# Attention scores as full-height products of stacked q and k, the mask within the row maximum, scores negated

## The chip, the cores and the metric

The kernel runs on one core of a Trainium2 chip. The metric is the device time of one execution in microseconds (us); for the kernel before, three timed executions gave a median of 1242.78 us (1242.35 to 1244.48). One further execution was taken with the hardware profiler; its own time was 1240.29 us. All rows below come from it. Engines are called TensorE (PE in the rows, PEld for its weight loads), VectorE (DVE), ScalarE (ACT), GpSimd (POOL) and SyncE (SP, which issues the transfers).

## The reference

The input is x, 512 positions by 1024 features, float32. Two layers follow, each an attention and a feed-forward network (SwiGLU, 2816 hidden features), each of these closed by `x <- LayerNorm(alpha * x + sublayer(x))`.

Layer A is differential attention with rotary positions: 8 heads, and in each head two maps of 64 features that share one value of 128 features.

```python
q = apply_rope(q, cos, sin) * (A_HEAD_DIM ** -0.5)
k = apply_rope(k, cos, sin)
sc = einsum('bqhmd,bkhmd->bhmqk', q[:, q0:kend], k[:, :kend])
allowed = chunk_id[None, :kend] <= chunk_id[q0:kend, None]      # chunks of 64
p = softmax(where(allowed, sc, neg), axis=-1)
a = p[:, :, 0] - lam * p[:, :, 1]
```

`a` is multiplied by the values, normalised (RMS) and projected. Layer B is chunked attention of 16 heads with 64 features; with 512 positions its band of nine chunks holds every key up to the end of the query's own chunk. A learned bias by relative distance is added to its scores before the softmax.

## The kernel before, in words

All float32 operands of the matrix products are split into a high part that TensorE takes (`F32R`) and a low part, what is left; a product is then high x high + high x low + low x high, three matmuls that add into one PSUM bank. The features lie on the partitions for q and k (128 of them: the two maps of a head of A, or two heads, a pair, of B), the positions along the free dimension.

The kernel has six stages one after the other: values and q, k of the first head; attention A; feed-forward 0; first projections of B; attention B; feed-forward 1. In either attention stage there are 32 units: 8 heads (or pairs, in B), each with 4 query tiles of 128 positions. A unit (`unit_a`, L978, and `unit_b`, L1218) makes the scores of both maps into a pair of PSUM banks (`scores`, L817), the row maximum (`top`), the exponential with its sum (`ex`), in A the combination of both maps (`mix`) and in B the division (`norm`), transposes the result on TensorE (banks of the tag `sm`) and multiplies it with the values.

Scores: a map has 64 features, so its q and k take half the partitions. `scores` runs over the three products and in each over the two maps, so that a matmul on partitions 0 to 63 and one on 64 to 127 follow one another, into two banks. A query tile reads keys up to its own end, but at least 256 columns: 256, 256, 384 and 512 for the four tiles. In A two more matmuls with one partition (`ind`, `negrow`) add a large negative number to the last 64 keys for the first 64 queries. In B the bias tile holds it already, and a fused VectorE instruction adds the bias, writes the sum to `e` and takes the maximum; a multiplication by -1 follows.

q and k of a head come from a projection (`qk_a`, L868: 24 matmuls of 512 columns each; `qk_b`, L1126). In A, `rope` copies the projection to `r`, swaps the halves with four transfers to `sw`, multiplies with cosine and sine, adds, and then `high` (ScalarE) and `low` (VectorE) write `qh`, `ql` or `kh`, `kl`; this last part begins when the units of the head before have begun. In B, `split_` does the two steps directly from PSUM; the bank (tag `pj`, two of them) is free when `low` has read it, and the output projection `o_proj` takes the same two banks when the projections are done.

Order of the work. Each engine executes its instructions in the order in which this program issues them, and a planner decides that order: `Modelled` and `Model` (L58, L97) keep an estimated clock for each engine and the estimated time at which each block of a tile is ready. `chain` issues a step on another engine when its inputs are estimated to be ready. `weave` (L243) interleaves the attention's steps with fill work, that is projections of later heads, values and the output projection: at each `fill` step a set time's worth of it (`FA`, `FB`), and, where a step waits for `there(...)`, as much as is estimated to pass until the tiles are there. In A the fill rates of the last three units are nearly zero. Weights come in chunks of 512 KB by SP (`fetch`, five raw buffers) and are split by ScalarE and VectorE (some by GpSimd) two chunks ahead of use.

Of the kernel before, what the change touches and what calls it, by code (L numbers as in the profile page):

```python
# [19 lines left out]
P = 128  # L20
S = 512
# [111 lines left out]
def trunk(ctx, tc, x, a_w_qkv, a_lambda, a_subln_g, a_w_o, kv_w, b_w_q, b_rel_bias, b_w_o,  # L133
# [212 lines left out]
    def fetch():  # L346

        i = state["raw"]
        if i < len(order):
            src, shape, _ = plan[order[i]]  # L350
            raws[i] = new(wraw, NRAW, [P] + shape, F32, "raw", f"raw_{order[i]}")
            load_e.dma_start(raws[i], src)
            state["raw"] += 1
# [463 lines left out]
    def scores(sc, q, k, qt, mask=True):  # L817
        kend = (qt + 1) * P
        N = max(kend, 256)
        qs = slice(qt * P, (qt + 1) * P)  # L820
        for i, (a, b) in enumerate(((0, 0), (0, 1), (1, 0))):
            for m in range(2):
                ms = slice(m * 64, (m + 1) * 64)
                mm(sc[m][:, :N], q[a][ms, qs], k[b][ms, :N], start=(i == 0), stop=(i == 2 and not mask))
        for m in range(2 if mask else 0):
            mm(sc[m][:, kend - 64:kend], ind, negrow, start=False, stop=True)
# [23 lines left out]
    ind = ap1.tile([1, P], BF16, name="ind")  # L850
    vec_e.memset(ind[:, 0:64], 1.0)
    vec_e.memset(ind[:, 64:P], 0.0)
    negrow = ap1.tile([1, 64], BF16, name="negrow")
    vec_e.memset(negrow, NEG)
# [13 lines left out]
    def qk_a(h):  # L868
# [4 lines left out]
        def rope(nm, scale, ps):  # L873
# [7 lines left out]
            out = {}  # L881

            def add():
                vec_e.tensor_add(rc, rc, sw)

            def high():
                out["h"] = new(ap2, 2, [P, S], F32R, nm + "h", f"{nm}h_{h}")
                act_e.activation(out["h"], rc, AF.Copy, scale=scale)

            def low():  # L890
                out["l"] = new(ap2, 2, [P, S], F32R, nm + "l", f"{nm}l_{h}")
                vec_e.scalar_tensor_tensor(out["l"], rc, scale, out["h"].bitcast(F32), op0=ALU.mult,
                                           op1=ALU.subtract)
# [13 lines left out]
        for nm, scale in (("q", SCALE), ("k", 1.0)):  # L907
# [4 lines left out]
            rope(nm, scale, ps)  # L912
# [65 lines left out]
    def unit_a(h, qt):  # L978
# [3 lines left out]
        q, k = qk[h]  # L982
        sc = pair(f"sc_{n_}")
        scores(sc, q, k, qt)
# [54 lines left out]
    def attention_a():  # L1039
# [3 lines left out]
        for i in range(nu + max(step[1] for step in STEPS if step[0] != "fill")):  # L1043
            rates = FA[0] if i < FA[2] else FA[1] if i < nu else FA[3]
            for kind, n in STEPS:
# [6 lines left out]
                if kind == "s":  # L1052
                    yield lambda: h in qk
                    yield lambda: there(*qk[h][0], *qk[h][1])
# [69 lines left out]
    oTl = oTp.tile([P, KT, S], F32R, name="oTl1")  # L1124

    def qk_b(p):  # L1126

        parts = [("bq", SCALE), ("bk", 1.0)]
        res = []

        def split_(nm, scale, ps):
            hi = new(bp2, 2, [P, S], F32R, nm + "h", f"{nm}h_{p}")
            lo = new(bp2, 2, [P, S], F32R, nm + "l", f"{nm}l_{p}")
            chain([hi, lo, ps], (lambda: [ps], lambda: act_e.activation(hi, ps, AF.Copy, scale=scale)), (
                lambda: [hi], lambda: vec_e.scalar_tensor_tensor(
                    lo, ps, scale, hi.bitcast(F32), op0=ALU.mult, op1=ALU.subtract)))
            res.append((hi, lo))

        if p == 0:
            ws = [take(f"{nm}{p}") for nm, _ in parts]  # L1140
            pss = [bank("pj", f"{nm}_ps_{p}") for nm, _ in parts]
# [234 lines left out]
```

## Time and profile before

| what | us |
|---|---|
| median of three runs (lowest to highest) | 1242.78 (1242.35 to 1244.48) |
| the profiled execution, its own time | 1240.29 |
| its span, first to last instruction | 1238.5 |
| TensorE busy | 1204.0 |
| VectorE busy | 888.7 |
| ScalarE busy | 526.3 |
| GpSimd busy | 454.6 |

The span lies inside the execution's time. A matmul's shown duration includes its way through the array, and matmuls overlap, so what a matmul costs is read from the distance between its start and the next start, not from its duration. A row of the timeline merges like instructions that follow one another without a gap; "x2" is their number, the second column the time from the first one's start to the last one's end.

### The profile page before, as it was taken

Reading aid. Unit: us, or ns where it says so; the run is one execution under the profiler, and the core shown is the slowest. Engines: PE = TensorE matmul, PEld = TensorE weight load, DVE = VectorE, ACT = ScalarE, POOL = GpSimd, SP = SyncE. Lnnn points to the kernel's source line nnn. Section 1 sums busy time; section 2 is a strip of 40 time slices with the busy share of each in tenths; the row PEclk is TensorE's granted clock in tenths of the full one; section 3 lists DMA queues with packets and bytes.
Section 4 is the critical chain, followed back from the end, with each engine's and each line's share of the span. In section 5 each row is a group of like instructions: output and inputs, shape, how many; then the busy total and the mean of one; then the engine's idle time right before and its main releaser. Section 6 shows DMA issues by size and latency. Waiting matters only on the chain.

```text
span 1238.5 us, 20141 instructions
## 1 busy us (share of the span) xinstructions
PE 1204.0 (97%) x7832; PEld 1070.5 (86%) x7832; DVE 888.7 (72%) x1386; ACT 526.3 (42%) x1009; POOL 454.6 (37%) x408
## 2 busy tenths in 40 slices
PE   8999999999999999999999999999999999999997
PEld 7878887788999999888897888878889999998886
DVE  4587576489999999432655677776899999983327
ACT  4356555333444444322235565563344444443220
POOL 0135333417666663001213232313186666620022
PEclk9999999899999999999999999999999999999999
DMA  8433222443554444523243222225423443353321
GB/s 263 112 87 108 65 75 85 150 128 94 151 143 136 134 125 136 171 88 133 85 137 115 73 86 86 69 86 187 120 68 107 118 117 103 103 174 116 102 68 68
DMA packets 161631, 141.56 MB, mean 114 GB/s; under 512 B 5584, under 2 KB 136944, under 8 KB 161536
## 3 DMA queue, kind: packets, MB, share of 16 engines
q1 hardware_dynamic: 161536, 140.28, 37.3%
q8 instruction: 61, 1.00, 0.3%
q14 instruction: 34, 0.28, 0.1%
HBM read 127.63 MB, written 13.67 MB: 114 GB/s over the span
## 4 chain that ended last, share of the span: by engine, by line
PE 81%; DVE 8%; POOL 4%; issue 3%; ACT 2%; DMA 1%; SPq 0%; DVEq 0%; POOLq 0%; ACTq 0%
PE m L194 29%; PE a L194 5%; PE b L194 5%; PE c L194 5%; PE d L194 4%; PE va_ps L194 4%; PE k_ps L194 3%; PE q_ps L194 3%; PE bq_ps L194 3%; PE vb_ps L194 2%; PE bk_ps L194 2%; PE sc L194 2%; POOL ha L75 2%; PE ob L194 2%; POOL sums L75 2%
## 5 line engine op out<-in xcount | busy, mean ns | idle before, releaser
L75 POOL TENSOR_TENSOR lo_fo<-raw_fo,hi_fo 128x1024 fp32r<-128x1024 f32 x8 | 19.1, 2392 | 215.4 <-ACT hi_fo L75 215.4
L75 POOL TENSOR_TENSOR sums<-raw_u 128x512 f32<-128x512 f32 x38 | 50.9, 1340 | 119.9 <-DVE s3lo L75 119.9
L75 DVE TENSOR_TENSOR lo_fk<-raw_fk,hi_fk 128x1024 fp32r<-128x1024 f32 x28 | 33.9, 1224 | 66.4 <-ACT hi_fk L75 66.4
L75 POOL TENSOR_TENSOR sums<-raw_g,raw_u 128x512 f32<-128x512 f32 x38 | 77.7, 2044 | 0.0
L75 ACT ACTIVATE sg<-sg 128x512 f32<-128x512 f32 x38 | 24.0, 633 | 125.9 <-DVE sg L75 125.9
L75 ACT CAST s3hi<-sums 128x1024 fp32r<-128x1024 f32 x38 | 40.0, 1052 | 77.2 <-POOL sums L75 77.2
L75 POOL TENSOR_TENSOR sums<-raw_g,sums 128x512 f32<-128x512 f32 x38 | 70.6, 1858 | 0.0
L75 DVE TENSOR_TENSOR alo<-raw_g,ahi 128x1024 fp32r<-128x1024 f32 x38 | 64.2, 1691 | 0.0
L75 ACT CAST hi_fk<-raw_fk 128x1024 fp32r<-128x1024 f32 x28 | 29.4, 1051 | 74.2 <-PE d L194 71.0
L75 DVE TENSOR_TENSOR ulo<-raw_u,uhi 128x512 fp32r<-128x512 f32 x38 | 58.7, 1546 | 0.0
L194 PE MATMUL m<-T,s1hi 128*128 128x256 f32 x304 | 56.4, 283 | 0.0
L75 ACT ACTIVATE e_b<-e_b,mx_b 128x128 f32<-128x128 f32 (+3 forms) x64 | 35.5, 557 | 47.8 <-DVE mx_b L75 47.8
L75 POOL TENSOR_TENSOR sums<-sums,raw_g 128x512 f32<-128x512 f32 x38 | 52.6, 1385 | 2.8
L75 ACT CAST s1hi<-sums 128x1024 fp32r<-128x1024 f32 x38 | 39.5, 1039 | 21.6 <-POOL sums L75 21.6
L75 DVE TENSOR_TENSOR s1lo<-sums,s1hi 128x1024 fp32r<-128x1024 f32 x38 | 48.2, 1270 | 0.0
L75 POOL TENSOR_SCALAR ms<-ms 128x1 f32<-128x1 f32 x32 | 10.3, 320 | 101.4 <-ACT sq L75 101.3
L194 PEld LDWEIGHTS m<-T,s1hi 128*128 128x128 f32 x304 | 47.5, 192 | 0.0
L75 DVE TENSOR_TENSOR s3lo<-sums,s3hi 128x1024 fp32r<-128x1024 f32 x38 | 46.1, 1213 | 0.1
L75 POOL TENSOR_TENSOR rs<-rs,mexp 128x1 f32<-128x1 f32 x16 | 15.8, 987 | 79.3 <-DVE rs L75 79.3
L75 ACT CAST hi_fo<-raw_fo 128x1024 fp32r<-128x1024 f32 x16 | 16.9, 1054 | 64.5 <-PE d L194 64.5
L194 PE MATMUL m<-T1h,s1hi 128*128 128x256 f32 x152 | 43.2, 284 | 0.0
L194 PE MATMUL m<-T1l,s1hi 128*128 128x256 f32 x152 | 43.2, 284 | 0.0
(606 smaller groups left out, 4771.0 us busy)
## 6 DMA issues: line engine op xcount, KB each, us to landing
raw_g<-in_ffn_w_in_dram SPq DMA_DIRECT2D x44, 512.0 KB, 4.1
raw_u<-in_ffn_w_in_dram SPq DMA_DIRECT2D x44, 512.0 KB, 5.2
raw_fk<-in_ffn_w_out_dram SPq DMA_DIRECT2D x28, 512.0 KB, 3.7
raw_fo<-in_ffn_w_out_dram SPq DMA_DIRECT2D x16, 512.0 KB, 3.7
skew<-extd SPq DMA_DIRECT2D x16, 320.0 KB, 5.9
raw_va<-in_a_w_qkv_dram SPq DMA_DIRECT2D x8, 512.0 KB, 4.2
raw_q<-in_a_w_qkv_dram SPq DMA_DIRECT2D x8, 512.0 KB, 5.1
raw_k<-in_a_w_qkv_dram SPq DMA_DIRECT2D x8, 512.0 KB, 4.4
```

Of the source, the lines that this page charges most:

```text
L75: return issue(*args, **kwargs)
L194: nc.tensor.matmul(out_, lhsT, rhs, start=start, stop=stop)
```

## The change

q and k are stacked. A tile `qs` of a head holds, for each map, the high part of q on that map's 64 partitions and the low part on the other 64; `ks` holds the high part of k on both halves, the second one copied there by a transfer. A third tile, one of the pair `lows`, holds the low part of k on the map's own half and zeros on the other, written once per stage. Then `qs` x `ks` is high x high + low x high, `qs` x `lows` is high x low, each a product over all 128 partitions: two matmuls for each map. The tiles of `lows` use the slots (`g`, `b` of `lnp`) which hold the layer norm's parameters at other times.

In A the mask becomes a tile of zeros with the large negative number in its corner, and the row maximum takes the fused form that B has. In both layers this form now multiplies by -1 and takes the minimum, so that the result is the negated maximum, and the exponential multiplies by -1 again. `fetch` settles what is pending on the buffer that it is about to reuse before it reads its own counter.

```diff
@@ -345,7 +345,10 @@
     def fetch():
-        i = state["raw"]
+        i = None
+        while i != state["raw"]:
+            i = state["raw"]
+            settle(slots.get((wraw.name, "raw"), [])[-NRAW:][:i >= NRAW])
         if i < len(order):
             src, shape, _ = plan[order[i]]
             raws[i] = new(wraw, NRAW, [P] + shape, F32, "raw", f"raw_{order[i]}")
@@ -814,16 +817,58 @@
...
-    def scores(sc, q, k, qt, mask=True):
-        kend = (qt + 1) * P
-        N = max(kend, 256)
+    HALVES = (slice(0, 64), slice(64, P))
+    def low_keys(name):
+        tiles = [lnp.tile([P, 2, S], F32R, tag=c, name=f"{name}_{c}") for c in "gb"]
+        for t_ in tiles:
+            for m in range(2):
+                pool_e.memset(t_[HALVES[1 - m], m, :].bitcast(F32), 0.0)
+        return tiles
+    def stack_q(q, src, scale):
+        def high():
+            for m in range(2):
+                act_e.activation(q[HALVES[m], m, :], src[HALVES[m]], AF.Copy, scale=scale)
+        def low():
+            for m in range(2):
+                vec_e.scalar_tensor_tensor(q[HALVES[1 - m], m, :], src[HALVES[m]], scale,
+                                           q[HALVES[m], m, :].bitcast(F32), op0=ALU.mult, op1=ALU.subtract)
+        return high, low
+    def stack_k(k, kl, src):
+        def high():
+            for m in range(2):
+                act_e.copy(k[HALVES[m], m, :], src[HALVES[m]])
+        def low():
+            for m in range(2):
+                load_e.dma_start(k[HALVES[1 - m], m, :].bitcast(F32), k[HALVES[m], m, :].bitcast(F32))
+            for m in range(2):
+                vec_e.tensor_sub(kl[HALVES[m], m, :], src[HALVES[m]], k[HALVES[m], m, :].bitcast(F32))
+        return high, low
+    def scores(sc, q, k, kl, qt):
+        N = max((qt + 1) * P, 256)
         qs = slice(qt * P, (qt + 1) * P)
-        for i, (a, b) in enumerate(((0, 0), (0, 1), (1, 0))):
-            for m in range(2):
-                ms = slice(m * 64, (m + 1) * 64)
-                mm(sc[m][:, :N], q[a][ms, qs], k[b][ms, :N], start=(i == 0), stop=(i == 2 and not mask))
-        for m in range(2 if mask else 0):
-            mm(sc[m][:, kend - 64:kend], ind, negrow, start=False, stop=True)
+        for m in range(2):
+            for i, k_ in enumerate((k, kl)):
+                mm(sc[m][:, :N], q[:, m, qs], k_[:, m, :N], start=(i == 0), stop=(i == 1))
+    def masked(sc, added, e, low, kend):
+        for m in range(2):
+            vec_e.tensor_tensor_reduce(
+                out=e[:, m, :kend], in0=sc[m][:, :kend], in1=added[m][:, HALF - kend:HALF],
+                scale=-1.0, scalar=3.0e38, op0=ALU.add, op1=ALU.min, accum_out=low[:, m:m + 1])
...
-    ind = ap1.tile([1, P], BF16, name="ind")
-    vec_e.memset(ind[:, 0:64], 1.0)
-    vec_e.memset(ind[:, 64:P], 0.0)
-    negrow = ap1.tile([1, 64], BF16, name="negrow")
-    vec_e.memset(negrow, NEG)
+    mask = ap1.tile([P, HALF], F32, name="mask")
+    pool_e.memset(mask, 0.0)
+    pool_e.memset(mask[0:64, HALF - 64:HALF], NEG)
+    lows = low_keys("kla")
...
-        def rope(nm, scale, ps):
+        def rope(nm, ps):
...
-            out = {}
-
             def add():
                 vec_e.tensor_add(rc, rc, sw)
-
-            def high():
-                out["h"] = new(ap2, 2, [P, S], F32R, nm + "h", f"{nm}h_{h}")
-                act_e.activation(out["h"], rc, AF.Copy, scale=scale)
-
-            def low():
-                out["l"] = new(ap2, 2, [P, S], F32R, nm + "l", f"{nm}l_{h}")
-                vec_e.scalar_tensor_tensor(out["l"], rc, scale, out["h"].bitcast(F32), op0=ALU.mult,
-                                           op1=ALU.subtract)
-                res[nm] = (out["h"], out["l"])
-                if "q" in res and "k" in res:
-                    qk[h] = (res["q"], res["k"])
             def begin():
                 if done["n"] < 4 * (h - 1):
                     return later(300, begin, rc)
-                chain([rc], (lambda: [rc], high), (lambda: [out["h"]], low))
+                st = new(ap2, 2, [P, 2, S], F32R, nm + "s", f"{nm}s_{h}")
+                if nm == "q":
+                    high, low = stack_q(st, rc, SCALE)
+                    res[nm] = [st]
+                else:
+                    high, low = stack_k(st, lows[h % 2], rc)
+                    res[nm] = [st, lows[h % 2]]
+                def last():
+                    low()
+                    if "q" in res and "k" in res:
+                        qk[h] = (*res["q"], *res["k"])
+                chain([rc, st], (lambda: [rc], high), (lambda: [st], last))
...
-        q, k = qk[h]
         sc = pair(f"sc_{n_}")
-        scores(sc, q, k, qt)
+        scores(sc, *qk[h], qt)
...
         def top():
-            for m in range(2):
-                vec_e.tensor_reduce(nm[:, m:m + 1], sc[m][:, :kend], axis=AX.X, op=ALU.max, negate=True)
+            masked(sc, (mask, mask), e, nm, kend)
         def ex():
             for m in range(2):
-                act_e.activation(e[:, m, :kend], sc[m][:, :kend], AF.Exp, bias=nm[:, m:m + 1],
+                act_e.activation(e[:, m, :kend], e[:, m, :kend], AF.Exp, scale=-1.0, bias=nm[:, m:m + 1],
                                      accum_out=s[:, m:m + 1])
...
+    lows = low_keys("klb")
     def qk_b(p):
-        parts = [("bq", SCALE), ("bk", 1.0)]
+        parts = ("bq", "bk")
         res = []
-        def split_(nm, scale, ps):
-            hi = new(bp2, 2, [P, S], F32R, nm + "h", f"{nm}h_{p}")
-            lo = new(bp2, 2, [P, S], F32R, nm + "l", f"{nm}l_{p}")
-            chain([hi, lo, ps], (lambda: [ps], lambda: act_e.activation(hi, ps, AF.Copy, scale=scale)), (
-                lambda: [hi], lambda: vec_e.scalar_tensor_tensor(
-                    lo, ps, scale, hi.bitcast(F32), op0=ALU.mult, op1=ALU.subtract)))
-            res.append((hi, lo))
+        def split_(nm, ps):
+            st = new(bp2, 2, [P, 2, S], F32R, nm + "s", f"{nm}s_{p}")
+            if nm == "bq":
+                high, low = stack_q(st, ps, SCALE)
+                res.append(st)
+            else:
+                high, low = stack_k(st, lows[p % 2], ps)
+                res.extend([st, lows[p % 2]])
+            chain([st, ps, res[-1]], (lambda: [ps], high), (lambda: [st], low))
...
-        q, k = qk[p]
         bias = biases[p]
         kend = (qt + 1) * P
         n_ = f"b{p}_{qt}"
         sc = pair(f"sc_{n_}")
-        scores(sc, q, k, qt, False)
+        scores(sc, *qk[p], qt)
...
         def top():
-            for m in range(2):
-                vec_e.tensor_tensor_reduce(
-                    out=e[:, m, :kend], in0=sc[m][:, :kend], in1=bias[m][:, HALF - kend:HALF],
-                    scale=1.0, scalar=-3.0e38, op0=ALU.add, op1=ALU.max, accum_out=mx[:, m:m + 1])
-            vec_e.tensor_scalar_mul(mx, mx, -1.0)
+            masked(sc, bias, e, mx, kend)
         def ex():
             for m in range(2):
-                act_e.activation(e[:, m, :kend], e[:, m, :kend], AF.Exp, bias=mx[:, m:m + 1],
+                act_e.activation(e[:, m, :kend], e[:, m, :kend], AF.Exp, scale=-1.0, bias=mx[:, m:m + 1],
                                      accum_out=s[:, m:m + 1])
...
```

## Rows read from the trace of the kernel before

**Rows 1.** The page: busy time of the engines (1), and the chain by engine (4)

```profile
PE 1204.0 (97%) x7832; PEld 1070.5 (86%) x7832; DVE 888.7 (72%) x1386; ACT 526.3 (42%) x1009; POOL 454.6 (37%) x408
...
PE 81%; DVE 8%; POOL 4%; issue 3%; ACT 2%; DMA 1%; SPq 0%; DVEq 0%; POOLq 0%; ACTq 0%
```

**Rows 2.** Windows: stretch, its length, busy us (instructions) of PE, PEld, DVE, ACT, POOL; clock; DMA

```profile
46.00:231.00 185.00, 180.19 (x1100) 144.41 (x1099) 125.88 (x280) 103.42 (x311) 64.56 (x112) 0.98 0.27 78
209.00:231.00 22.00, 18.15 (x100) 13.63 (x100) 10.92 (x33) 10.84 (x39) 5.46 (x18) 0.84 0.00 1
659.00:845.00 186.00, 181.33 (x1108) 148.93 (x1108) 134.93 (x363) 109.18 (x291) 53.97 (x91) 1.00 0.25 77
```

**Rows 3.** Waits of TensorE, 46 to 231 us: us in total, times, longest

```profile
PE at L199 <- DVE oTl L75: 4.5, 5, 1.4
```

**Rows 4.** Waits of TensorE, 659 to 845 us

```profile
PE po L194 <- DVE ptl L75: 3.3, 3, 2.4
PE ob L194 <- DVE bkl L75: 0.7, 1, 0.7
```

**Rows 5.** Timeline of TensorE around one score group of A: start, us, instruction, number

```profile
50.89 0.40 PE L194 MATMUL q_ps<-xTh_a,lo_q 128*128 128x512 f32 x1
...
52.26 0.39 PE L194 MATMUL q_ps<-xTl_a,hi_q 128*128 128x512 f32 x1
```

**Rows 6.** Timeline of TensorE around one score group of B, 256 columns

```profile
748.71 0.40 PE L194 MATMUL bq_ps<-xTh_b,lo_bq 128*128 128x512 f32 x1
749.04 0.39 PE L194 MATMUL sc_b<-bkh,bqh 64*128 64x256 f32 x2
...
749.59 0.50 PE L194 MATMUL bq_ps<-xTh_b,hi_bq 128*128 128x512 f32 x1
749.92 0.40 PE L194 MATMUL bq_ps<-xTl_b,hi_bq 128*128 128x512 f32 x1
```

**Rows 7.** Timeline of TensorE, a full-height value product behind projection matmuls

```profile
730.97 0.28 PE L194 MATMUL vb_ps<-lo_vb,xTh_b 128*128 128x256 f32 x1
731.09 0.29 PE L194 MATMUL vb_ps<-hi_vb,xTl_b 128*128 128x256 f32 x1
731.22 0.40 PE L194 MATMUL po<-pth,vs 128*128 128x512 f32 x1
731.46 0.40 PE L194 MATMUL po<-ptl,vs 128*128 128x512 f32 x1
```

**Rows 8.** Timeline of TensorE, a score group of B with 512 columns

```profile
835.25 0.50 PE L194 MATMUL sc_b<-bkh,bqh 64*128 64x512 f32 x2
...
836.14 0.50 PE L194 MATMUL ob<-hi_ob,oTh 128*128 128x512 f32 x1
```

**Rows 9.** Tile views: duration ns min/median/max, first and last start; transfers: issue, and landing us

```profile
L75 ACT COPY tl<-po x16: 578/584/586, 685.9 to 849.0; 64x512 f32<-64x512 f32 x16
L75 DVE TENSOR_TENSOR ot<-po,tl x16: 667/682/685, 686.6 to 849.6; 64x512 f32<-64x512 f32 x16
...
L75 DVE TENSOR_REDUCE nm<-sc x64: 280/486/692, 47.4 to 223.3; 128x1 f32<-128x128 f32 x16, 128x1 f32<-128x256 f32 x16, 128x1 f32<-128x384 f32 x16, 128x1 f32<-128x512 f32 x16
...
L75 DVE CUSTOM_DVE_ANT_0 e_b<-sc_b,bias x64: 281/484/689, 660.4 to 838.0; 128x128 f32<-128x128 f32 x16, 128x256 f32<-128x256 f32 x16, 128x384 f32<-128x384 f32 x16, 128x512 f32<-128x512 f32 x16
...
L75 POOL MEMSET pth<- x16: 197/209/348, 661.4 to 828.9; 128x128 f32 x16
...
L92 SPq DMA_DIRECT2D ksw<-kr x32: 507/583/1608, 35.5 to 201.8; - x32
...
DMA to landing us min/median/max: 1.9/2.0/4.0
```

**Rows 10.** Timeline of all engines, the last head of A: its keys and first scores

```profile
207.07 0.63 ACT L75 ACTIVATE kh<-krc 128x512 fp32r<-128x512 f32 x1 [2.77 <-DVE krc L75]
...
208.16 0.68 DVE L75 SCALAR_TENSOR_TENSOR kl<-krc,kh 128x512 fp32r<-128x512 f32 x1
...
209.57 0.38 PE L194 MATMUL sc<-kh,qh 64*128 64x256 f32 x2
```

**Rows 11.** Timeline, GpSimd's first instruction of layer B, its idle time in brackets

```profile
643.24 2.40 POOL L75 TENSOR_TENSOR lo_bk<-raw_bk,hi_bk 128x1024 fp32r<-128x1024 f32 x1 [17.89 <-ACT hi_bk L75]
```

More of the change, by code (lines that the diff above doesn't have):

```diff
@@ L905, in rope @@
                   (lambda: [], begin))
-        for nm, scale in (("q", SCALE), ("k", 1.0)):
+        for nm in "qk":
             w = take(f"{nm}{h}")
@@ L911, in qk_a @@
             free(f"{nm}{h}")
-            rope(nm, scale, ps)
+            rope(nm, ps)
     extd = dram.tile([HB, EXT], F32, name="extd")
@@ L1053, in attention_a @@
                     yield lambda: h in qk
-                    yield lambda: there(*qk[h][0], *qk[h][1])
+                    yield lambda: there(*qk[h])
                     live[i] = [unit_a(h, qt), None]
@@ L1124, in trunk @@
     oTl = oTp.tile([P, KT, S], F32R, name="oTl1")
+    lows = low_keys("klb")
     def qk_b(p):
-        parts = [("bq", SCALE), ("bk", 1.0)]
+        parts = ("bq", "bk")
         res = []
-        def split_(nm, scale, ps):
-            hi = new(bp2, 2, [P, S], F32R, nm + "h", f"{nm}h_{p}")
-            lo = new(bp2, 2, [P, S], F32R, nm + "l", f"{nm}l_{p}")
-            chain([hi, lo, ps], (lambda: [ps], lambda: act_e.activation(hi, ps, AF.Copy, scale=scale)), (
-                lambda: [hi], lambda: vec_e.scalar_tensor_tensor(
-                    lo, ps, scale, hi.bitcast(F32), op0=ALU.mult, op1=ALU.subtract)))
-            res.append((hi, lo))
+        def split_(nm, ps):
[7 more added lines that the diff above has]
+            chain([st, ps, res[-1]], (lambda: [ps], high), (lambda: [st], low))
         if p == 0:
-            ws = [take(f"{nm}{p}") for nm, _ in parts]
-            pss = [bank("pj", f"{nm}_ps_{p}") for nm, _ in parts]
+            ws = [take(f"{nm}{p}") for nm in parts]
+            pss = [bank("pj", f"{nm}_ps_{p}") for nm in parts]
             for lo in (0, S // 2):
-                for w, ps, (nm, _) in zip(ws, pss, parts):
+                for w, ps, nm in zip(ws, pss, parts):
                     now(feature_major(ps[:, lo:lo + S // 2], w, lo, lo + S // 2))
@@ L1147, in qk_b @@
                 yield True
-            for (nm, scale), ps in zip(parts, pss):
-                split_(nm, scale, ps)
+            for nm, ps in zip(parts, pss):
+                split_(nm, ps)
         else:
-            for nm, scale in parts:
+            for nm in parts:
                 w = take(f"{nm}{p}")
@@ L1157, in qk_b @@
                     yield True
-                split_(nm, scale, ps)
+                split_(nm, ps)
         qk[p] = res
@@ L1303, in attention_b @@
                     yield lambda: p in qk
-                    yield lambda: there(*qk[p][0], *qk[p][1], *biases[p])
+                    yield lambda: there(*qk[p], *biases[p])
                     live[i] = [unit_b(p, qt), None]
```

## The prediction, made before the changed kernel was run

> **What bounds the kernel now.** I read the page first: TensorE is busy for 1204.0 of 1238.5 us, VectorE for 72%, and TensorE holds 81% of the chain that ended last [rows 1]. So the kernel is bound by TensorE's instruction stream, and what an edit is worth must be read where it acts: the two attention stages. The windows view of these (46 to 231 us for layer A, 659 to 845 us for layer B) shows TensorE busy 97% of either, VectorE 68% and 73%, ScalarE 56% and 59% [rows 2]. The waits view then asks whether TensorE stands still there. In A it does for 4.5 us in all, five times, always a transpose waiting for VectorE's `oTl` [rows 3]; these lie in the last four units (209 to 231 us), where no other work is left to fill in, and after them the granted clock of that stretch is 0.84 on average, a fall from 2.4 to 1.2 GHz for part of it [rows 2]. In B it is 3.3 us on `ptl` and 0.7 us on the last key projection's bank [rows 4]. The rest of both stages is matmul after matmul, so a matmul removed there is time removed.
>
> The timeline shows what the scores cost. A projection matmul of 512 columns starts 0.23 us after the one before it. A score group in A (256 columns) stands between a projection matmul at 50.89 and the second one behind it at 52.26: 1.37 us; less two projection steps of 0.23, the group takes 0.91 us [rows 5]. In B the same bracket is 748.71 to 749.92, 1.21 us, so 0.75 us [rows 6]. "x2" in one row of 0.39 us (749.04) says that the two half-height matmuls (64 partitions each, one per map) run side by side. Full-height matmuls of 256 columns start 0.12 us apart (730.97 to 731.09) [rows 7]. Three pairs at this pace would be 0.35 us. So B's group has 0.40 us on top, A's has 0.56 us. In B it sits at the edges: 748.71 to 749.04 is 0.33 in place of 0.23; inside, 749.04 to 749.59 is 0.55 in place of 0.35; the matmul at 749.59 takes 0.33 in place of 0.23 [rows 6]: four edges of 0.10. A 512-column unit has the same inner excess, 0.89 in place of 0.69 [rows 8], so I take it as independent of width. A's further 0.16 is the pair of mask matmuls.
>
> Is it the half height, or would any short group pay it? The value products of B, full-height, with weights and a bank of their own, stand between projection matmuls too: the projection step before them is 731.09 to 731.22, 0.13 us, and their own first step (512 columns) 731.22 to 731.46, 0.24 us: no edge [rows 7]. The Trainium skill, "TensorEngine Tiling (Array Packing)", Key Properties, says the like from the other side: changing the tiling mode drains the array. With these rows it puts the 0.40 us on the switch between half and full height, which the change abolishes.
>
> **The change part by part.**
> 1. Scores. Per unit, three pairs plus edges become four full-height matmuls in a row: gain = excess minus one more column pass. The pass is 0.12, 0.12, about 0.17 and 0.23 us for the four query tiles (256, 256, 384, 512 columns; the third interpolated), mean 0.16. In A 0.56 - 0.16 = 0.40 us, times 32 units: 12.8 us. In B 0.40 - 0.16 = 0.24, times 32: 7.7 us. Together 20.5 us. Bounds: if the edges stay, the loss is worked out in the first rival; if the four run as those projections do, 20.5.
> A rule that speaks against it: "TensorE: Matmul & The Clock Gate", section "Why this matters for your kernels", in the Trainium skill, advises to slice small contractions onto distinct row groups because they then run concurrently, and puts the gain in this concurrency. The change does the reverse; by that rule alone each unit gets one pass longer. The x2 rows agree that concurrency is real; only the edges turn the sign.
> 2. Splitting q and k. Each of the 32 tensors (q and k, 8 heads and 8 pairs) had one ScalarE and one VectorE operation on 128 x 512; it now has two of each on 64 x 512. Half the partitions cost as much as all: ScalarE `tl` 64x512 takes 0.584 us, VectorE `ot` 64x512 0.682 [rows 9], against 0.63 and 0.68 for the whole [rows 10]. So ScalarE gets 16 x 0.6 = 10 us more per stage, VectorE 16 x 0.68 = 11 us. VectorE's share in A goes to (125.9 + 10.9) / (185 - 12.8) = 79%. It is beside TensorE's work, but queues lengthen: 1.5 us lost, bounds 0 and 5 (half of what is added in A).
> 3. The copy of high k: two transfers of 128 KB on SP per head. Nearest: the rotary swap's copies, 0.58 us of issue, landing 1.9 to 4.0 us after it, median 2.0 [rows 9]. SP waits there for ScalarE, and weight loads stand behind it; they are fetched up to five chunks ahead, so 0, and one uncovered wait of 2 us at worst. Now the scores of head 7 start at 209.57, 0.7 us behind the end of its `kl` (208.16 + 0.68), whose chain begins with `kh` at 207.07 [rows 10]. Changed, the two halves end at 208.3, the second copy lands 2.0 to 2.6 us later, at 210.3 to 210.9: 0.8 to 1.4 us after the present start, while TensorE comes there some 0.8 us earlier (two units). So a wait of 1.6 to 2.2 us. The planner (`there`) puts projection work in front of it where it has some. I take 2.0 us for all eight heads together, bounds 0 and 8 (four such waits).
> 4. End of B. The output projection waits 0.7 us for the bank of the last keys, until `bkl` has read it [rows 4]. One more ScalarE half (0.58) and one more VectorE half (0.68) lie before that: 1.3 us more. Bounds 0 (other work stands there) and 2.6 (queued behind both engines).
> 5. Row maximum and exponential. A's reduction (median 486 ns) becomes B's fused form (484) with a short read behind it, and B loses a small multiplication per unit [rows 9]: both about nothing, off TensorE. The maximum of map 0 may start two matmuls earlier, for its bank is now ready first. Bounds for the tail below: 0 to 0.2 us per unit, either way.
> 6. Tail of A. In the last four units the chain through VectorE and ScalarE sets the pace [rows 3], so their 4 x 0.40 us need not all show: 0.8 lost, bounds 0 and 1.6.
> 7. Memsets of low k (four of 64 x 512 at each stage's start) and of the mask, on GpSimd. Nearest: 128x128 in 0.21 us [rows 9], so 0.2 to 0.84 each (four times the columns). Before B's first use GpSimd idles for 17.9 us [rows 11]; the start of A is alike. 0; 3.4 us if that cover were gone. The loop in `fetch` issues nothing: 0.
>
> Sum: 20.5 - 1.5 - 2.0 - 1.3 - 0.8 = 14.9 us. The profiled execution took 1240.29 us (span 1238.5): 1225.4. The median shown, 1242.78, lies 2.5 above it, so 1228.
>
> **The rivals.**
> - *The edges stay* (slower). If the 0.40 us belonged to any score group (new weights for every matmul, another bank), a unit would pay 0.40 + 4 passes: in A nothing is gained (0.16 of mask against 0.16 of a pass), in B 32 x 0.16 = 5.1 us are lost, and the 5.6 us of items 2, 3, 4 and 6 come on top: 1251.0, median 1253.5. For it: the extra pass is certain, and no row shows a full-height score; it is what the Trainium skill's rule of item 1 comes to in this kernel. Against: the value products [rows 7]. It decides once more than 0.23 us of the 0.40 stay ((20.5 - 5.6) / 64).
> - *The late copies give it back.* Four or five heads wait 2.2 us each with nothing to fill in, 10 us in place of 2.0, and the clock may fall after such a wait as it did behind the tail. 1225.4 + 8 = 1233.4, median 1236; up to 3.5 more (0.16 of 22 us, rows 2) with such a fall. For it: head 7's margin [rows 10]. Against: the planner waits by its own estimate and pulls other matmuls forward.
> - *All of it shows.* Everything added hides: 1240.3 - 20.5 = 1219.8, median 1222; near 1219 if also the clock's fall at the tail shrinks.
> - *VectorE becomes the bound in A* at 79%: of A's 12.8 us half is lost, 5 us more than taken: 1230.4, median 1233.
>
> **How the numbers follow.** Forecast 0.51 (its own range 1223 to 1233), all of it shows 0.20, late copies 0.15, edges stay 0.08, VectorE 0.06. A measurement of this kernel tells about 0.2% (2.5 us) from no change. Faster: 0.51 + 0.20 + 0.06 + 0.10 of the late copies = 0.87; no change 0.04 and slower 0.01 from the rest of these; slower with the edges 0.09. The range reaches from below the best case to the late copies with a fall of the clock: 1217 to 1240; outside are the edges and a little at either end.
>
> **What would show it.** Right: in the timeline a score group is four full-height matmuls, 0.12 or 0.23 us apart, without a longer step before or behind; the stages end about 10 and 6 us earlier; `ob` waits some 2 us for `bkl`. Wrong: score steps longer by 0.1 (edges stay); TensorE waiting for `ks` or its copies in the waits view (late copies); waits for `lo` tiles of weights (VectorE). Were the stages shorter and the end not, the prediction's premise, a bound by TensorE alone, would be wrong.

## The result, and the profile after

The changed kernel takes 1250.07 us (median of 14 runs, 1244.65 to 1254.12), the kernel before 1242.86 (14 runs, 1239.91 to 1244.62). The ratio is 1.0057, interval 1.0044 to 1.0070: slower by 7.2 us, where 14.9 us of gain were forecast. Its profiled execution took 1247.45 us, span 1245.7.

The page of the kernel after, parts 1 and 4, answers to [rows 1]: TensorE is busy for 9.5 us less and the span is 7.2 us longer. So TensorE now stands still more.

```profile
PE 1194.5 (96%) x7640; PEld 1080.1 (87%) x7640; DVE 892.4 (72%) x1447; ACT 552.3 (44%) x1041; POOL 453.9 (36%) x418
...
PE 80%; DVE 7%; POOL 4%; issue 4%; ACT 3%; DMA 1%; SPq 0%; DVEq 0%; ACTq 0%; POOLq 0%
```

The windows of the kernel after, the stretches and columns of [rows 2]. TensorE's busy share fell from 97% to 90% in A (166.90 of 185) and to 96% in B, with a granted clock of 0.96 where it had been 0.98.

```profile
46.00:231.00 185.00, 166.90 (x934) 141.32 (x933) 135.03 (x348) 110.93 (x312) 62.79 (x105) 0.96 0.32 87
209.00:231.00 22.00, 16.95 (x80) 13.23 (x79) 14.57 (x45) 11.34 (x37) 6.38 (x15) 0.84 0.23 63
659.00:845.00 186.00, 177.94 (x1044) 155.51 (x1043) 127.24 (x342) 118.57 (x303) 52.45 (x92) 0.99 0.32 96
```

The scores themselves became as cheap as forecast. The timeline of TensorE in the kernel after (start, us, instruction), one group of A and one of B of 256 columns, answers to [rows 5, 6]:

```profile
74.69 0.40 PE L194 MATMUL q_ps<-xTh_a,lo_q 128*128 128x512 f32 x1
74.92 0.28 PE L194 MATMUL sc<-ks,qs 128*128 128x256 f32 x1
...
75.27 0.28 PE L194 MATMUL sc<-kla_b,qs 128*128 128x256 f32 x1
75.39 0.83 PE L194 MATMUL o<-va,aT 128*128 128x128 f32 x6
...
691.21 0.28 PE L194 MATMUL vb_ps<-hi_vb,xTl_b 128*128 128x256 f32 x1
691.33 0.28 PE L194 MATMUL sc_b<-bks,bqs 128*128 128x256 f32 x1
...
691.68 0.28 PE L194 MATMUL sc_b<-klb_b,bqs 128*128 128x256 f32 x1
691.80 0.28 PE L194 MATMUL vb_ps<-hi_vb,xTh_b 128*128 128x256 f32 x1
```

Each group is four steps of about 0.12 us (74.92 to 75.39, 691.33 to 691.80: 0.47 us) with a plain step before it (0.23 and 0.12): no edges. Over all undisturbed groups the time that a unit's scores take in the stream (start to start, less its neighbours' own steps) fell in A from 0.91, 1.09 and 1.26 us (256, 384, 512 columns) to 0.48, 0.71 and 0.94, and in B from 0.76, 0.93 and 1.09 to 0.48, 0.72 and 0.94. Times 32 units each, that is 12.5 and 7.3 us: 19.8 us of matmul time gone.

It came back as waits. The waits of TensorE in the kernel after (us in total, times, longest), first 46 to 231 us, then 640 to 850 us:

```profile
PE at L199 <- DVE oTl L75: 12.3, 11, 3.7
PE o L194 <- ACT aT L75: 3.2, 3, 2.4
PE sc L194 <- DMA ks<-ks: 1.8, 1, 1.8
...
PE pt_b L199 <- DVE ot L75: 3.2, 5, 1.0
PE ob L194 <- DVE klb_b L75: 2.1, 1, 2.1
PE pt_b L199 <- DVE e_b L75: 1.6, 1, 1.6
PE pt_b L199 <- DVE ptl L75: 0.9, 2, 0.7
```

Against [rows 3], A's transposes now wait 12.3 us for `oTl` instead of 4.5, and not only in the tail; the waits for `aT` and for the transfer are new. Against [rows 4], the stall on `po` is gone and others took its place. With every gap above 0.1 us counted, TensorE stands still for 18.1 us in A (before: 4.8) and 9.8 in B (before: 6.5).

By stage, divided where the first scores, the first feed-forward matmul and B's first projection start, A takes 225.6 us (before 219.6), feed-forward 0 takes 356.4 (354.9), and B with its first projections 256.6 (257.5). With a first score that comes 0.6 us later, these make up the 7.2 us.

Where such a wait comes from is seen in the timeline of the kernel after, 80 to 85 us (in brackets: idle before, releaser):

```profile
80.24 0.27 PE L199 MATMUL ot<-ident,sq 128*128 128x128 f32 x1
...
80.60 1.26 ACT L75 CAST ks<-krc 64x512 fp32r<-64x512 f32 x2 [1.57 <-DVE krc L75]
...
81.24 1.14 SPq L92 DMA_DIRECT2D ks<-ks  x2
81.25 1.40 DVE L75 TENSOR_TENSOR kla_g<-krc,ks 64x512 fp32r<-64x512 f32 x2
81.88 0.51 ACT L75 ACTIVATE e<-e,nm 128x256 f32<-128x256 f32 x1
...
83.22 0.25 ACT L75 CAST oTh<-ot 128x128 fp32r<-128x128 f32 x1
...
83.86 0.28 DVE L75 TENSOR_TENSOR oTl<-ot,oTh 128x128 fp32r<-128x128 f32 x1
...
84.20 0.33 PE L199 MATMUL at<-ident,e 128*128 128x128 f32 x1 [3.69 <-DVE oTl L75]
```

The transpose `at` at 84.20 needs one of the two `sm` banks; `ot` holds one until `oTh` (ScalarE) and then `oTl` (VectorE) have read it. `ot` was written at 80.24. ScalarE first does the two halves of the next head's high keys (80.60, 1.26 us), and only then, from 81.88, two exponentials, the square `sq` and `oTh`; `oTl` follows these. VectorE does the two halves of the low keys meanwhile (81.25, 1.40 us). The second half on ScalarE is 0.63 of the 3.69 us for which TensorE stands still; the rest shows because the order has no projection matmul between `ot` and `at` to fill the time: 36 of them had been pulled in front of head 1's scores (66.55 to 74.92 us).

Then the clock falls. Windows of the kernel after (columns as above; the last but two is the granted clock), and below them the first of these stretches in the kernel before:

```profile
84.20:90.00 5.80, 5.80 (x22) 4.64 (x23) 3.46 (x11) 2.45 (x9) 1.27 (x5) 0.71 0.01 3
119.00:124.00 5.00, 4.35 (x24) 4.35 (x25) 4.90 (x13) 3.67 (x9) 0.00 (x0) 0.66 0.26 59
826.00:830.00 4.00, 4.00 (x17) 3.72 (x18) 2.01 (x6) 1.01 (x4) 0.00 (x0) 0.57 0.39 134
```

```profile
84.20:90.00 5.80, 5.80 (x33) 4.41 (x32) 5.04 (x9) 3.39 (x8) 2.04 (x4) 1.00 0.28 81
```

The clock is on average 0.71, 0.66 and 0.57 in these stretches, where the first has 1.00 before: part of each runs at 1.2 GHz. The stalls just ahead of them are the 3.69 us at 84.20, 1.89 us at 119.65 (again `at`) and 2.09 us at 825.91 (`ob`). In all, and without the last microseconds of the kernel, the kernel after spends 23.9 us at the lower level, the one before 10.2; at half speed that is up to some 7 us lost (an estimate from these two). The runs of the kernel after also spread more (9.5 us against 4.7); the one with a mean clock of 0.993 had a span of 1242.9 us, the four with 0.985 had 1250.6 to 1252.3.

### The profile page after: what moved, and what is told of

Its sections match the earlier page's. It is cut to its first block, busy times and chain, and to the rows that moved or that the text cites. A ratio compares the mean times of both kernels' runs of the same rounds, so it can differ in the third digit from the quotient of the medians.

```text
span 1245.7 us, 19973 instructions
## 1 busy us (share of the span) xinstructions
PE 1194.5 (96%) x7640; PEld 1080.1 (87%) x7640; DVE 892.4 (72%) x1447; ACT 552.3 (44%) x1041; POOL 453.9 (36%) x418
## 4 chain that ended last, share of the span: by engine, by line
PE 80%; DVE 7%; POOL 4%; issue 4%; ACT 3%; DMA 1%; SPq 0%; DVEq 0%; ACTq 0%; POOLq 0%
PE m L194 29%; PE c L194 5%; PE a L194 5%; PE b L194 5%; PE d L194 4%; PE vb_ps L194 4%; PE bk_ps L194 3%; PE va_ps L194 3%; PE bq_ps L194 3%; PE q_ps L194 2%; PE k_ps L194 2%; POOL ha L75 2%; PE sc_b L194 2%; PE po L194 2%; PE pt_b L199 2%
## 5 line engine op out<-in xcount | busy, mean ns | idle before, releaser
L75 POOL TENSOR_TENSOR sums<-raw_g,sums 128x512 f32<-128x512 f32 x38 | 75.4, 1983 | 0.0
L75 POOL TENSOR_TENSOR sums<-raw_g,raw_u 128x512 f32<-128x512 f32 x38 | 68.8, 1810 | 0.0
L75 DVE TENSOR_TENSOR alo<-raw_g,ahi 128x1024 fp32r<-128x1024 f32 x38 | 68.3, 1798 | 0.0
L75 DVE TENSOR_TENSOR ulo<-raw_u,uhi 128x512 fp32r<-128x512 f32 x38 | 48.8, 1285 | 0.0
L194 PE MATMUL m<-T1h,s1lo 128*128 128x256 f32 x152 | 43.3, 285 | 0.0
```

The lines of the kernel that those rows point to most:

```text
L75: return issue(*args, **kwargs)
L194: nc.tensor.matmul(out_, lhsT, rhs, start=start, stop=stop)
```

## The experiments

Every kernel below was timed in five rounds against the kernel before on the same chip (medians of before: 1243.8 for the first group, up to `e4_copy_on_act`, 1243.4 and 1243.2 for the next two). Ratios are to it, with their interval. Differences between kernels are of medians; worked out from the ratios they come out within 0.6 us of these, for `e1_half_height` 1.3 us smaller.

**Is the score gain real?** `e1_half_height` is the kernel after with half-height score pairs.

```diff
-        for m in range(2):
-            for i, k_ in enumerate((k, kl)):
-                mm(sc[m][:, :N], q[:, m, qs], k_[:, m, :N], start=(i == 0), stop=(i == 1))
+        for i in range(3):
+            for m in range(2):
+                k_ = kl if i == 1 else k
+                h_ = HALVES[m]
+                mm(sc[m][:, :N], q[h_, m, qs], k_[h_, m, :N], start=(i == 0), stop=(i == 2), cost=2 / 3)
```

> The changed kernel with its new preparation of q and k, but scores as half-height pairs again (three pairs a unit; the third repeats high x high in place of low q x high k, so this part is left out). The planner is told the same score time as in the changed kernel, so the order of instructions is that of the changed kernel. It prices the full height alone: 0.24 us a unit, 64 units, 15.4 us. Theory 'late preparation' (the copies come late, the planner spends fill work ahead of heads 1, 5 and 7 and has none later): TensorE's score time still counts where it is not idle, 1256 to 1265. Theory 'VectorE and ScalarE load': the same, 1256 to 1265. Theory 'chain-bound' (the attention stages are not bound by TensorE, so score time is hidden): 1248 to 1252, as the changed kernel.

Measured: 1262.61 us, 1.0147 (1.0126 to 1.0168), 12.5 us over the kernel after. Full height is worth 12.5 of item 1's 15.4 us also inside the new kernel, so a bound by other engines alone is out.

**Each half of item 1 on the old kernel.** `e2_mask_alone` is the kernel before with the mask in the row maximum and the negated scores; the split and the half-height matmuls are the old ones.

```diff
-        scores(sc, q, k, qt)
+        scores(sc, q, k, qt, False)
...
-                vec_e.tensor_reduce(nm[:, m:m + 1], sc[m][:, :kend], axis=AX.X, op=ALU.max, negate=True)
+            masked(sc, (mask, mask), e, nm, kend)
```

> The kernel before with only the mask moved into the row maximum and the scores negated; old split of q and k, half-height scores. It takes the two mask matmuls, 0.16 us a unit in A, 5.1 us in all, and B's small multiplication. 'Late preparation' and 'load': 1243 - 5 = 1236 to 1240. 'Chain-bound': 1243, within 2.

Measured: 1233.00 us, 0.9912 (0.9897 to 0.9927): 10.8 us faster, more than expected, and the fastest kernel here that computes everything. In the traces A shrinks by 4.1 us (219.6 to 215.5) and B, whose matmuls are unchanged, by 4.0 (257.5 to 253.5). B's waits on `po` [rows 4] are gone; its row maximum lost a small VectorE multiplication per unit, which I had put at nothing (that, and the sign in the exponential, were not tried apart). The other 2.7 us are not located: the two profiles differ by only 6.5 us, and that of before (1240.29) was among its fastest runs.

`e3_old_split_full` adds full-height products on the old, unstacked tiles.

```diff
-        for i, (a, b) in enumerate(((0, 0), (0, 1), (1, 0))):
-            for m in range(2):
-                ms = slice(m * 64, (m + 1) * 64)
-                mm(sc[m][:, :N], q[a][ms, qs], k[b][ms, :N], start=(i == 0), stop=(i == 2 and not mask))
+        for m in range(2):
+            for i in range(2):
+                mm(sc[m][:, :N], q[i][:, qs], k[i][:, :N], start=(i == 0), stop=(i == 1))
```

> As e2_mask_alone, but the scores are four full-height matmuls a unit on the unstacked q and k (high x high and low x low over all 128 partitions, so the two maps are mixed: the separation of the maps and the cross products are left out). It has the changed kernel's score time with the old preparation. 'Late preparation' and 'load': the whole 20.5 us less about 2: 1222 to 1227. 'Chain-bound', or the planner's new order by itself: 1238 or more.

Measured: 1223.56 us, 0.9846 (0.9829 to 0.9863), 20.2 us under the kernel before. This is items 1 and 5 without items 2 to 4, and it has item 1's size. So what the kernel after loses lies in how q and k are prepared.

**The copies.** `e4_copy_on_act` lets ScalarE write the second copy of the high keys, in place of the transfers.

```diff
+            for m in range(2):
+                act_e.copy(k[HALVES[1 - m], m, :], src[HALVES[m]])
...
-            for m in range(2):
-                load_e.dma_start(k[HALVES[1 - m], m, :].bitcast(F32), k[HALVES[m], m, :].bitcast(F32))
```

> The changed kernel, but ScalarE writes the second copy of high k itself (two more 64x512 operations) in place of the two transfers. The chain of a head's keys ends 1.3 us later on ScalarE, but 2 to 3 us of transfer go. 'Late preparation': a part comes back, 1243 to 1248. 'Load': ScalarE has 10 us more per stage, 1250 to 1254.

Measured: 1246.61 us, 1.0031 (1.0013 to 1.0049): 3.5 us better than after, still slower than before. That is what late preparation foretold; the next runs show that the copies are the smaller part. `e5_no_copy` has no copies at all: the high keys lie in tiles whose other half is zero.

```diff
-                load_e.dma_start(k[HALVES[1 - m], m, :].bitcast(F32), k[HALVES[m], m, :].bitcast(F32))
...
-                st = new(ap2, 2, [P, 2, S], F32R, nm + "s", f"{nm}s_{h}")
+                st = new(ap2, 2, [P, 2, S], F32R, nm + "s", f"{nm}s_{h}") if nm == "q" else owns[h % 2]
```

> The changed kernel without the transfers that copy high k: the other half of each key tile is zero, written once a stage (low q x high k is left out). Splitting in halves, full-height scores, low keys as in the changed kernel. 'Late copies' (what costs is that the copies land late, with the planner's answer to that): most of the 26 us between the changed kernel and e3_old_split_full come back, 1228 to 1236. 'Halves' (twice as many instructions on ScalarE and VectorE are what costs): little comes back, 1245 to 1250.

Measured: 1241.29 us, 0.9985 (0.9975 to 0.9996). The copies cost 8.8 us, and without them the kernel is still 17.7 us from `e3_old_split_full`; the time lies between the two ranges expected. `e6_blind` leaves the copies but the planner doesn't hear of them.

```diff
-                load_e.dma_start(k[HALVES[1 - m], m, :].bitcast(F32), k[HALVES[m], m, :].bitcast(F32))
+                nc.sync.dma_start(k[HALVES[1 - m], m, :].bitcast(F32), k[HALVES[m], m, :].bitcast(F32))
```

> The changed kernel with the copies as they are, but the planner is not told of them: it takes the keys as ready when ScalarE and VectorE are done, pulls less fill work ahead of a head, and TensorE waits itself where a copy is late. 'The planner's answer costs' (fill spent ahead, none later): 1236 to 1244. 'The lateness itself costs': 1248 to 1256, with waits for the copies of 2 to 3 us at several heads.

Measured: 1246.20 us, 1.0023 (1.0012 to 1.0033). So 3.9 of the 8.8 us come from the order that the planner chose because of the copies, and this is net: TensorE now waits for copies five times, 3.1 us in all, where it did so once for 1.8. This time, too, lies between the ranges expected.

**More room in the schedule.** `e8_ahead` projects head 1 ahead of the first scores, head 7 ahead of the last values, and gives less fill per step.

```diff
-FA = ((750.0, 2250.0, 600.0), (0.0, 0.0, 1150.0), 29, (1100.0, 900.0, 900.0))
+FA = ((680.0, 2000.0, 500.0), (0.0, 0.0, 1150.0), 29, (1100.0, 900.0, 900.0))
...
+    now(qk_a(1))
```

> The changed kernel, whole, with head 1 of A projected ahead of the attention stage, head 7 ahead of the last values, and the fill rates of A lowered in proportion (from 3.6 to 3.18 us a unit). 'Late copies': A has no late head 1 and less late head 7, 8 to 10 us of A's 14 come back: 1238 to 1243. 'Halves': 1247 to 1251.

Measured: 1246.20 us, 1.0023 (1.0015 to 1.0032): 3.9 us of the 7.2 come back, again between the ranges. Having the heads' q and k earlier doesn't restore the gain.

**The halves.** `e7_halves` is `e3_old_split_full` with the splits in two halves, without copies.

```diff
-                act_e.activation(out["h"], rc, AF.Copy, scale=scale)
+                for m in range(2):
+                    hs = slice(m * 64, (m + 1) * 64)
+                    act_e.activation(out["h"][hs], rc[hs], AF.Copy, scale=scale)
```

> e3_old_split_full (full-height scores on the old tiles, maps mixed, cross products left out) with each split of q and k in two halves of 64 partitions on ScalarE and VectorE, no copies. 'Halves': 1236 to 1246. 'Late copies': 1224 to 1229, as e3_old_split_full plus 1 to 4.

Measured: 1242.34 us, 0.9996 (0.9975 to 1.0016): 18.8 us above `e3_old_split_full`, and within 1.1 us of `e5_no_copy`, which comes from the other side. Nothing else in the edit differs: the halves take the whole gain. A part of the 18.8 us goes with the clock: the six runs with a mean granted clock of 0.991 to 0.994 have a median of 1238.3 us, 14.7 above `e3_old_split_full`, the six with 0.984 to 0.989 took 1243.6 to 1248.0. How the halves act, the last group asks. `e9_halves_untold` issues the same halves, but the planner hears of the first ones only.

```diff
-                    act_e.activation(out["h"][hs], rc[hs], AF.Copy, scale=scale)
+                    (nc.scalar if m else act_e).activation(out["h"][hs], rc[hs], AF.Copy, scale=scale)
```

> e7_halves (full-height scores on the old tiles, maps mixed, cross products left out, splits in halves), with the planner told of the first half of each split only, so that the work is ordered as in e3_old_split_full. 'The planner's answer' (later estimated keys, so another order of the fill work, is what the halves cost): 1224 to 1230. 'Engine load' (the added instructions delay VectorE and ScalarE): 1238 to 1245, as e7_halves.

Measured: 1238.63 us, 0.9965 (0.9954 to 0.9977), 15.1 us above `e3_old_split_full`. The order of all other instructions on the four compute engines is the same in the two traces: what is added is 32 instructions each on ScalarE and VectorE, and these alone cost the 15.1 us. This is the run that shows the cause. `e10_told_only` is the reverse, single instructions for which the planner charges double.

```diff
+    def charged(eng, src):
+        eng.free_at = max(eng.free_at, model.ready(src)) + eng.fixed + eng.each * S
+        return eng
...
-                act_e.activation(out["h"], rc, AF.Copy, scale=scale)
+                charged(act_e, rc).activation(out["h"], rc, AF.Copy, scale=scale)
```

> e3_old_split_full (maps mixed, cross products left out) with single splits, but the planner is told that each takes twice as long, so that the work is ordered as in e7_halves. 'The planner's answer': 1236 to 1243. 'Engine load': 1222 to 1227.

Measured: 1230.78 us, 0.9899 (0.9884 to 0.9915): 7.2 us for another order alone, between the ranges of both theories. The order isn't quite that of `e7_halves`: of 7640 matmuls 62 stand elsewhere, 85 against `e3_old_split_full`. So what `e7_halves` owes to its own order stays open; its runs at the higher clock (14.7) leave nothing for it beside the 15.1. `e12_halves_act` splits in halves on ScalarE only.

```diff
-                for m in range(2):
-                    hs = slice(m * 64, (m + 1) * 64)
-                    vec_e.scalar_tensor_tensor(out["l"][hs], rc[hs], scale, out["h"][hs].bitcast(F32),
-                                               op0=ALU.mult, op1=ALU.subtract)
+                vec_e.scalar_tensor_tensor(out["l"], rc, scale, out["h"].bitcast(F32), op0=ALU.mult,
+                                           op1=ALU.subtract)
```

> e7_halves with the halves on ScalarE only, VectorE's splits whole (maps mixed, cross products left out). If VectorE's load is what costs: 1225 to 1231. If ScalarE's load or the planner's answer to 0.5 us more: 1234 to 1242.

Measured: 1234.54 us, 0.9935 (0.9919 to 0.9951): ScalarE's halves cost 11.0 us, VectorE's another 7.8, each with the planner's answer to them (against `e3_old_split_full` 67 matmuls stand elsewhere, against `e7_halves` 77). `e11_untold`, last, is the kernel after with a planner that hears neither of the second halves nor of the copies.

```diff
-                act_e.copy(k[HALVES[m], m, :], src[HALVES[m]])
+                (nc.scalar if m else act_e).copy(k[HALVES[m], m, :], src[HALVES[m]])
```

> The changed kernel, whole, with the planner told neither of the second halves nor of the copies. 'The planner's answer': 1228 to 1236, and it would beat the kernel before. 'Engine load' and lateness itself: 1243 to 1250.

Measured: 1244.36 us, 1.0013 (0.9998 to 1.0028): 5.7 us better than after, not better than before. Another order mends a part; no run here takes the load away and still computes everything with full-height scores.

**Where the load acts.** The waits of TensorE in `e3_old_split_full`, 46 to 235 and then 640 to 850 us:

```profile
PE at L199 <- DVE oTl L75: 6.5, 8, 1.3
PE o L194 <- ACT aT L75: 0.8, 2, 0.6
...
PE pt_b L199 <- DVE ot L75: 1.3, 2, 0.9
PE ob L194 <- DVE bkl L75: 0.7, 1, 0.7
```

and in `e9_halves_untold`:

```profile
PE at L199 <- DVE oTl L75: 9.0, 10, 2.2
PE o L194 <- ACT aT L75: 5.0, 4, 3.1
...
PE pt_b L199 <- DVE ot L75: 2.2, 2, 1.8
PE ob L194 <- DVE bkl L1150: 2.1, 1, 2.1
```

These four grow by 2.5, 4.2, 0.9 and 1.4 us, 9.0 of the 10.3 us by which TensorE's idle time in the two stages grows (8.6 to 15.9 and 4.1 to 7.1). Some 3.2 us more lie in the feed-forward stages (356.5 against 354.9, 353.9 against 352.3), where nothing was changed. Time at 1.2 GHz is the same in both kernels (10.2 us), but not its place. Windows of 7 us around two waits of TensorE in feed-forward 0 (2.5 and 1.8 us long where both are seen), first in `e3_old_split_full`, then in `e9_halves_untold`:

```profile
302.00:309.00 7.00, 6.26 (x40) 6.26 (x41) 6.17 (x6) 2.21 (x4) 5.02 (x3) 0.76 0.55 164
314.00:321.00 7.00, 6.71 (x57) 6.53 (x56) 6.90 (x8) 3.44 (x5) 5.29 (x4) 1.00 0.38 109
```

```profile
310.40:317.40 7.00, 6.29 (x52) 6.29 (x53) 6.16 (x6) 2.18 (x4) 5.05 (x3) 1.00 0.59 174
322.40:329.40 7.00, 6.32 (x40) 6.36 (x41) 6.90 (x8) 3.50 (x5) 5.22 (x4) 0.76 0.41 111
```

The clock falls at the first wait in the one, at the second in the other. The traces of all 14 kernels hold 28 feed-forward stages. In the 12 where it falls at the second wait, feed-forward 0 takes 356.4 to 356.5 us and feed-forward 1 353.8 to 353.9; in the other 16, where it falls at the first or not at all, they take 354.9 to 355.0 and 352.3 to 352.4. So these 3.2 us go with the place of the fall, and so do the 1.5 us that the kernel after loses in feed-forward 0. What decides at which wait it falls was not tested.

The largest single step, 3.1 us, comes at the same matmul of both traces. The timeline of `e9_halves_untold`:

```profile
159.60 2.41 POOL L75 TENSOR_TENSOR lo_va<-raw_va,hi_va 128x1024 fp32r<-128x1024 f32 x1 [0.23 <-ACT hi_va L75]
...
159.91 2.67 DVE L75 TENSOR_TENSOR krc<-krc,ksw 128x512 f32<-128x512 f32 x1
...
162.61 0.63 ACT L75 ACTIVATE kh<-krc 64x512 fp32r<-64x512 f32 x1 [3.08 <-DVE krc L75]
163.26 0.63 ACT L895 ACTIVATE kh<-krc 64x512 fp32r<-64x512 f32 x1
...
163.91 0.37 ACT L75 COPY aT<-at 128x256 f32<-128x256 f32 x1
...
164.34 0.71 PE L194 MATMUL o<-va,aT 128*128 128x128 f32 x4 [3.13 <-ACT aT L75]
```

and of `e3_old_split_full`:

```profile
154.14 0.68 DVE L75 TENSOR_TENSOR krc<-krc,ksw 128x512 f32<-128x512 f32 x1
154.20 2.86 POOL L75 TENSOR_TENSOR lo_va<-raw_va,hi_va 128x1024 fp32r<-128x1024 f32 x1 [0.85 <-ACT hi_va L75]
...
154.85 0.63 ACT L75 ACTIVATE kh<-krc 128x512 fp32r<-128x512 f32 x1 [0.73 <-DVE krc L75]
...
155.39 0.35 ACT L75 COPY aT<-at 128x256 f32<-128x256 f32 x1
```

In one, `krc` starts 0.06 us before GpSimd's `lo_va` and takes 0.68 us; in the other it starts 0.31 us after it and takes 2.67. `kh` waits for `krc`, `aT` stands behind `kh` on ScalarE, and behind the second half besides (0.65 us), and TensorE waits for `aT`. So of this stall the added instruction itself is the smaller part; that the queues stand in another alignment is the larger one. That a two-operand instruction of VectorE stretches beside GpSimd was read from traces, not tested by a run of its own.

## Why the prediction was wrong

**What bounds the kernel: half right.** TensorE is the bound as long as every helper is in time. I took 97% busy for the proof, and the short list of waits [rows 3, 4] for the absence of others; it only shows which had not yet come late. The two attention stages had just 4.8 and 6.5 us of idle time, and that was no sign of plenty of room: 64 short instructions beside TensorE cost 15.1 us (`e9_halves_untold`). The waits of A, too, lie not all in the last four units: three of the five do, 3.8 of the 4.5 us.

**Item 1: right in sum, in part by luck.** 20.5 us forecast, 20.2 measured (`e3_old_split_full`), 19.8 in the traces' matmul steps. The measured sum is that of two misses which cancel, 5.7 us too much and 6.0 too little. The mask gave 10.8 in place of 5.1: B, whose row maximum (item 5) was taken as nothing, gave back 4.0. Full height then gave 9.4 in place of 15.4, while TensorE's idle time in the two stages rose (from 8.4 to 12.7 us). The rule on small contractions that the prediction cites from the Trainium skill, "TensorE: Matmul & The Clock Gate", "Why this matters for your kernels", doesn't decide in this kernel's short groups: half height costs 12.5 us more than full height (`e1_half_height`). "The edges stay" came near in time (1253.5), but its mechanism is refuted by the same runs.

**Item 2: this is the step that failed.** The durations were right (ScalarE 0.62 us for half the partitions, VectorE 0.69), and so was their sum, 41 us of engine time in both stages. The text then said that "queues lengthen: 1.5 us lost, bounds 0 and 5"; it was 18.8 (`e7_halves`, its clock included), and 15.1 without any change of order (`e9_halves_untold`). I reasoned by the share of VectorE, 79% foreseen, 73% in the window of A after. A share can't answer this. What had to be asked is which instructions stand behind each added half on its engine, and how long TensorE can do without them: `oTh` and `oTl` free one of only two `sm` banks, `aT` feeds the next value product, and both come once per unit. The bound of 5 was a share of the load as well; a bound by this mechanism would have been both engines' added time in full.

**Item 3: the copy, 2.0 taken, 8.8 measured**, just outside its bounds of 0 and 8. Head 7 waits for its copy as foreseen (1.8 us, forecast 1.6 to 2.2), and only that head does so. Of the rest, 3.9 us are the planner's own answer (`e6_blind`), which pulls projections forward in front of head 1 and leaves later units bare, as at 84.20; what is left was not taken apart. I had counted `there` as the cover that hides the wait, and not what the moved fill was then missing from.

**Items 4, 6 and 7.** `ob` waits 2.1 us for the last keys, 2.0 forecast. The memsets of the low keys take 0.52 us each; those of B lie at 635 us, before anything needs them, those of A at 2.0 us. The first scores come 0.6 us later (46.7 for 46.1), which isn't shown to be theirs: without them `e3_old_split_full` has its first score at 47.5. The tail of A can't be read apart, since it now holds head 7's late copy and the units moved.

**The clock** was foreseen as an addition to one rival (up to 3.5 us). It became a term of its own, up to about 7 us (an estimate, from the time at 1.2 GHz): the waits ahead of its falls are now spread over the stages and not gathered in the tail. No run sets the clock apart from the stalls.

**The balance**: 20.2 gained, 18.8 lost to the halves, 7.7 to the copies (the kernel after against `e7_halves`), part of both by way of the clock: 6.3 us slower, against 7.2 by the pair measured together; the medians of before differ by 0.9 between the groups of runs. The chance of 0.09 for slower was hung on the edges almost alone (0.08). The four losses were added as small independent terms; those of items 2, 4 and 6 act on the same two queues.

## What to carry to other kernels

Before adding work to an engine that is "only" two thirds busy, list what stands behind the new instructions in its queue and, for each, the bank or operand that the bounding engine waits for next, with the number of buffers and the time until it is needed; the share of busy time says nothing on this. Where a planner orders the work, try the edit also with the planner not told of it, so that load and order are priced apart. And take a change apart before judging it: here the mask with the negated scores is by itself 0.9% faster (`e2_mask_alone`), while the whole is slower.

## What the runs showed of the hardware

- An instruction on half of the partitions cost as much as one on all: ScalarE 0.62 us (64 x 512, kernel after) against 0.63, VectorE 0.69 against 0.68 [rows 10]. Splitting by partitions doubled the price.
- An addition of VectorE with two operands in SBUF stretched beside a tensor operation of GpSimd. `krc` took 2.67 us where it started after `lo_va` and 0.68 where it started before it (the seven other `krc` of `e9_halves_untold`, none beside a `lo_va`, took 0.68 or 0.69); it ended at 162.58, 0.57 us after `lo_va` (162.01). The Trainium skill, "SBUF — State Buffer", section "SBUF: two separate sides", describes an exclusive lock on a pair of ports that the two engines share, held for a whole instruction by the one that starts first. The trace agrees in either order: in `e3_old_split_full` `krc` was first, and `lo_va` took 2.86 us in place of 2.41.
- Full-height score matmuls had no edges against other full-height work (0.12 us per step of 256 columns, behind plain steps of 0.23 and 0.12), where half-height groups had four of 0.10 us [rows 6].
- The granted clock fell to 1.2 GHz at six places of the kernel after and at two of the kernel before (the very end left out). At all six lies a wait of TensorE of 1.8 to 3.7 us: five end up to 1.5 us ahead of the fall, and the sixth, of 2.53 us, ends just behind it (the fall is at 928.6). Of the two before, the one at 309.0 lies within such a wait too (2.53 us), the one at 220.2 at the end of three shorter ones (0.98 to 1.44). But one such wait alone doesn't decide it: 2.4 us for `ptl` before [rows 4] and 3.13 us at 164.34 in `e9_halves_untold` brought no fall. And a fall need not cost time: at the first wait of the feed-forward stages it cost nothing, at the second 1.5 us.

```profile
928.71 0.58 PE L194 MATMUL m<-T_1l,uhi 128*128 128x256 f32 x1 [2.53 <-DVE T_1l L75]
```
